# Dense products in runs of twelve, a perturbed planner, and two small edits on VectorE: one layer of a hybrid encoder on one core

## The chip, the cores and the metric

The kernel runs on one core of one Trainium2 chip. The time is device microseconds of that core. It is one launch; its engines are TensorE (PE, with its weight loads PEld), VectorE (DVE), ScalarE (ACT), GpSimd (POOL) and SyncE (SP), which issues the DMAs.

## What is computed

One layer for 1024 prompt rows and 32 sample rows (1056 columns in all), model width 1024, everything in float32. Cut to what matters:

```python
n = rmsnorm(x, norm_mix);  p = n @ w_in                  # 1024 -> 3840 columns: HGRN2 | RWKV-7
hg_o = hgrn2(p[..., :2048]);  rw_o = rwkv7(p[..., 2048:])  # the two mixers, with states
x = x + concat(hg_o, rw_o) @ w_out
x = x + cross_attend(rmsnorm(x), mk, mv) @ w_co          # mk, mv: 256 memory rows
x = x + (silu(n @ w_ff1) * (n @ w_ff3)) @ w_ff2          # n = rmsnorm(x), width 2816
y = rmsnorm(x, norm_final)
# rwkv7 begins with a shift by one row:  xs = p + (prev - p) * mu,  prev = row before
```

## The kernel before, in words

The activations lie transposed, features on the 128 partitions and the 1056 rows along the free axis, in three blocks of 352 columns.

**Dense products.** A float32 product is made of three float32r products: activations and weights are each split into a rounded part and a rest (hi, lo), and hi·hi, hi·lo and lo·hi are summed in one PSUM bank (`gemm`, line 864). `load_w` (line 850) fetches a weight tile, ScalarE rounds it (a CAST into the region `rw`), and GpSimd or VectorE subtracts to get the rest. The feed-forward stage uses seven products of sub-blocks instead of eight (`fast`, line 1252), 264 columns wide.

**The mixers.** Each 128-column tile of the projection is a dense product of 24 matmuls per block; for the 14 RWKV tiles `rw_proj` (line 1542) mixes each row with the one before it while it empties the bank. The first column of a block needs the last column of the block before, kept in a one-column tile `edge`. The mixers then work on chunks with many small products (64x64, or 128x128 blocks of which the halves are separate), between which VectorE, ScalarE and GpSimd do element-wise work; the triangular inverse (`inverse`, line 1814) is a chain of some twenty such products per piece of 256 rows.

**What sets the order.** Nothing is issued in the order of the code. The calls are recorded as nodes of a graph (`record`, line 335). Consecutive TensorE calls form one node, until `cut()` is called: `gemm` and `fast` call it every `CUT` steps of k, so a dense node has 3 x `CUT` matmuls. `plan` (line 448) is a list scheduler: it gives each node a price and walks a clock per engine, taking the ready node with the best rank; `fits` checks that tiles of SBUF (in pages of 66 words, in the regions f0, r0, rw, wr, mb, r1) and PSUM banks are there. `latest` plans backwards, and its result is the rank of the next pass. The result is one fixed order for each engine. All instructions are issued from one line of `emit`, so every row of the profile has line L378 (L383 in the changed kernel); operations are told apart by their tiles: `bank` is a PSUM bank, `rw` holds rounded weights, `wr` and `r` raw weights or rounded activations, `mb` and `f` the tiles of the mixers and other float32 tiles.

Of the kernel before, what the change touches and what calls it, by code (L numbers as in the profile page):

```python
# [33 lines left out]
CUT = 2  # L34
WARM = 2.0
LATER = 10.0
PASSES = 3
# [25 lines left out]
RESERVE = [64, 32, 24, 24, 24, 24, 24]  # L63
# [137 lines left out]
class Engine:  # L201
# [3 lines left out]
    def __getattr__(self, method):  # L205
        return lambda *args, **kw: self.graph.record(self.name, method, args, kw)

# [90 lines left out]
class Graph:  # L298
# [90 lines left out]
    def order(self):  # L389
# [7 lines left out]
        base = {n: n.cost for n in self.nodes}  # L397
        bufs = list(dict.fromkeys(b for n in self.nodes for b in n.bufs))
        best, rank = None, None
        self.log = []  # L400
        for _ in range(PASSES):
            for n in self.nodes:
                n.cost = base[n]
                if n.unit:
                    n.unit[2] = 0
            for b in bufs:
                b.at = None
            try:
                out = self.plan(rank)
            except AssertionError:  # L410
                self.log.append(None)
                break
            self.log.append(self.span)
            if best is None or self.span < best[0]:
                best = self.span, out, [b.at for b in bufs], [(n.start, n.cost) for n in self.nodes]
            rank = self.latest(out)
        self.span = best[0]
        for b, at in zip(bufs, best[2]):
            b.at = at
        for n, t in zip(self.nodes, best[3]):  # L420
            n.start, n.cost = t
        return best[1]
# [25 lines left out]
    def plan(self, rank):  # L448
# [29 lines left out]
        for n in nodes:  # L478
            n.path = n.path - n.bias if rank is None else -rank[n]
        engines = ("tensor", "vector", "scalar", "gpsimd", "sync")  # L480
        clock = dict.fromkeys(engines, 0.0)
        warm = 0.0
# [79 lines left out]
        def fits(n, start):  # L562
# [9 lines left out]
            for c in FIFO:  # L572
                k = sorted(b.turn for b in new if b.cls == c)
                if k and (k != list(range(turn[c], turn[c] + len(k))) or live[c] + len(k) > FIFO[c]):
                    return None
            ps = sum(b.space == "PS" for b in new)
            if ps:
                free = sorted(t for t in banks if t < BIG)
                if len(free) < ps + (0 if first else 2):
# [40 lines left out]
        while len(done) < len(nodes):  # L620
            turn_over()
            best = None
            for e in engines:
# [7 lines left out]
                lack = e == "tensor" and now - warm > WARM  # L631
                for t, n in sorted(ready[e], key=lambda r: (max(r[0], now), lack and not r[1].dense, -r[1].path)):
# [29 lines left out]
            if e == "tensor" and n.dense:  # L662
                warm = clock[e]
# [1389 lines left out]
```

## Time and profile before

| | |
|---|---|
| time, median of 3 runs | 1875.8 us (1875.39 to 1876.47) |
| the profiled execution's own time | 1872.31 us |
| its span, first to last instruction | 1870.6 us |
| mean granted TensorE clock | 0.988 |
| PE busy | 1798.7 us, 96% |
| VectorE, ScalarE, GpSimd busy | 69%, 44%, 32% |

The stages lie in the span like this: the input rows and first projections until about 100 us, the mixers until about 718 with the memory's keys and values behind them until 782, the output projection and cross-attention until 1136, the feed-forward hidden part until about 1600, the feed-forward output and the final norm after that. PE's busy time counts a matmul from its start to its modelled end, so a busy PE can still be switching between kinds of products or running at a lower clock.

### The profile page before, as it was taken

Reading aid. Unit: us, or ns where it says so; the run is one execution under the profiler, and the core shown is the slowest. Engines: PE = TensorE matmul, PEld = TensorE weight load, DVE = VectorE, ACT = ScalarE, POOL = GpSimd, SP = SyncE. Lnnn points to the kernel's source line nnn. Section 1 sums busy time; section 2 is a strip of 40 time slices with the busy share of each in tenths; the row PEclk is TensorE's granted clock in tenths of the full one; section 3 lists DMA queues with packets and bytes.
Section 4 is the critical chain, followed back from the end, with each engine's and each line's share of the span. In section 5 each row is a group of like instructions: output and inputs, shape, how many; then the busy total and the mean of one; then the engine's idle time right before and its main releaser. Section 6 shows DMA issues by size and latency. Waiting matters only on the chain. (4 is left out here: it accounts for less than half of the span.)

```text
span 1870.6 us, 39378 instructions
## 1 busy us (share of the span) xinstructions
PE 1798.7 (96%) x15439; PEld 1689.5 (90%) x15439; DVE 1287.8 (69%) x2547; ACT 827.0 (44%) x1938; POOL 594.7 (32%) x764
## 2 busy tenths in 40 slices
PE   6899999999999999999999999999999999999898
PEld 5898888888788888999999999899999999999897
DVE  5347746887766678623654547798877777978997
ACT  5535527465454567633322346333333333653432
POOL 6234234354323433245000024523223223233321
PEclk9999999999999999999999999999999999999999
DMA  6364123222312136844111143133222224644622
GB/s 190 103 193 113 37 79 100 81 69 64 101 49 66 61 101 193 248 139 137 47 46 46 48 149 103 46 113 123 87 94 90 87 102 169 202 146 141 194 69 94
DMA packets 206314, 201.88 MB, mean 108 GB/s; under 512 B 18712, under 2 KB 191376, under 8 KB 206128
## 3 DMA queue, kind: packets, MB, share of 16 engines
q1 hardware_dynamic: 206128, 199.37, 34.3%
q8 instruction: 121, 1.98, 0.5%
q14 instruction: 65, 0.53, 0.1%
HBM read 139.66 MB, written 59.67 MB: 107 GB/s over the span
## 5 line engine op out<-in xcount | busy, mean ns | idle before, releaser
L378 PE MATMUL bank<-r,rw 128*128 128x264 f32 (+1 forms) x5952 | 927.6, 308 | 8.9 <-DVE mb L378 4.1
L378 PEld LDWEIGHTS bank<-r,rw 128*128 128x128 f32 x5952 | 844.8, 189 | 26.6 <-issue 4.6
L378 PE MATMUL bank<-mb,rw 128*128 128x264 f32 (+2 forms) x3648 | 516.9, 296 | 17.3 <-DVE f L378 6.1
L378 PEld LDWEIGHTS bank<-mb,rw 128*128 128x128 f32 x3648 | 486.9, 190 | 25.3 <-ACT rw L378 5.7
L378 DVE TENSOR_TENSOR f<-bank,f 128x264 f32<-128x264 f32 (+6 forms) x541 | 239.6, 459 | 206.3 <-PE bank L378 167.5
L378 DVE TENSOR_TENSOR f<-f 128x264 f32<-128x264 f32 (+8 forms) x348 | 221.6, 656 | 19.1 <-POOL f L378 7.6
L378 POOL TENSOR_TENSOR f<-f 128x64 f32<-128x64 f32 (+8 forms) x237 | 128.0, 553 | 323.4 <-ACT f L378 265.2
L378 ACT CAST rw<-wr 128x512 fp32r<-128x512 f32 (+3 forms) x162 | 113.0, 705 | 242.4 <-PE bank L378 209.3
L378 PE MATMUL bank<-f 128*128 128x128 f32 (+12 forms) x1244 | 185.6, 291 | 2.5 <-DVE f L378 1.0
L378 ACT ACTIVATE f<-f 128x256 f32<-128x256 f32 (+6 forms) x331 | 142.0, 452 | 101.2 <-DVE f L378 47.9
L378 DVE TENSOR_TENSOR mb<-bank,f 128x1024 f16<-128x1024 f32 (+6 forms) x203 | 144.5, 735 | 43.8 <-PE bank L378 33.5
L378 PEld LDWEIGHTS bank<-f 128*128 128x128 f32 (+7 forms) x1244 | 141.7, 160 | 28.1 <-issue 5.5
L378 PE MATMUL bank<-f,mb 128*128 128x64 f16 (+5 forms) x2264 | 121.4, 216 | 25.5 <-POOL f L378 13.9
L378 ACT CAST rw<-r 128x512 fp32r<-128x512 f32 (+2 forms) x128 | 73.3, 574 | 121.9 <-PE bank L378 84.5
L378 ACT COPY mb<-bank 128x512 f32<-128x512 f32 (+5 forms) x175 | 76.7, 455 | 112.7 <-PE bank L378 93.6
L378 DVE TENSOR_TENSOR rw<-r,rw 128x512 fp32r<-128x512 f32 (+2 forms) x128 | 93.4, 733 | 38.0 <-ACT rw L378 37.6
L378 DVE TENSOR_TENSOR rw<-wr,rw 128x512 fp32r<-128x512 f32 (+3 forms) x132 | 102.3, 779 | 14.5 <-ACT rw L378 13.1
L378 ACT COPY f<-bank 128x264 f32<-128x264 f32 (+4 forms) x233 | 72.8, 336 | 88.7 <-PE bank L378 77.0
L378 POOL TENSOR_TENSOR r<-r 128x512 f32<-128x512 f32 (+2 forms) x45 | 66.9, 1493 | 131.9 <-DVE rw L378 67.6
L378 POOL TENSOR_TENSOR rw<-wr,rw 128x1024 fp32r<-128x1024 f32 x30 | 73.2, 2450 | 101.2 <-ACT rw L378 73.1
L378 PE MATMUL bank<-mb 64*64 64x64 f32 (+4 forms) x1556 | 84.5, 236 | 5.0 <-DVE mb L378 4.0
L378 PEld LDWEIGHTS bank<-f,mb 64*64 64x64 f32 (+3 forms) x1176 | 54.5, 139 | 34.5 <-POOL f L378 14.1
(117 smaller groups left out, 1661.6 us busy)
## 6 DMA issues: line engine op xcount, KB each, us to landing
wr<-in_w_in_dram SPq DMA_DIRECT2D x30, 512.0 KB
p_scratch<-mb SPq DMA_DIRECT2D x83, 176.0 KB
wr<-in_w_ff_dram SPq DMA_DIRECT2D x27, 512.0 KB
r<-in_w_ff_dram SPq DMA_DIRECT2D x25, 512.0 KB
f<-h_scratch SPq DMA_DIRECT2D x46, 264.0 KB
h_scratch<-f SPq DMA_DIRECT2D x17, 528.0 KB
h_scratch<-f SPq DMA_DIRECT2D x19, 396.0 KB
f<-x_scratch SPq DMA_DIRECT2D x14, 528.0 KB
```

The costliest lines, as they stand in the source:

```text
L378: getattr(eng, method)(*args, **kw)
```

## The change

Four things change.

- `CUT` goes from 2 to 4: a dense node has twelve matmuls where it had six.
- The planner: it no longer prefers a dense node when TensorE has gone more than 2 us of its clock without one (`WARM`); it no longer keeps two banks back for the oldest node; it keeps 16 pages back in the first two phases instead of 64 and 32; it makes one pass for ranks and then plans with ranks that are perturbed by fixed pseudo-random numbers (`shake`, `nudged`), instead of taking the best of three passes. `START` perturbs the first pass in the same way; each entry of `NUDGE` is a time, a seed and a reach: nodes from that time on get their rank moved by up to the reach.
- The four products `rkj` (a 128x128 constant times a per-partition factor) move from VectorE to ScalarE.
- In `rw_proj` the first column of a block is made by ScalarE alone: it scales the bank's column and adds `edge`, which now holds the previous block's last column already multiplied by `mu`. VectorE's one-column operations fall away. For the sample rows the factor is made once (`msh`, one small product).

```diff
-CUT = 2
-WARM = 2.0
+CUT = 4
-PASSES = 3
+PASSES = 1
+START, NUDGE = (291, 0.5), ((0, 3825, 0.6), (480, 1426, 0.2), (660, 4358, 1.5), (720, 1344, 0.6), (840, 6345, 3), (1200, 2280, 1.5), (1560, 9149, 3), (1620, 5315, 0.2), (1680, 6266, 12), (1740, 8928, 1.5),)
-RESERVE = [64, 32, 24, 24, 24, 24, 24]
+RESERVE = [16, 16, 24, 24, 24, 24, 24]
+def shake(i, seed):
+    return (i * 2654435761 + seed * 40503 * 65537 >> 7) % 1021 / 1020 if seed else 0.0
...
-        for _ in range(PASSES):
...
-            if best is None or self.span < best[0]:
-                best = self.span, out, [b.at for b in bufs], [(n.start, n.cost) for n in self.nodes]
-            rank = self.latest(out)
...
+        rank = None
+        for _ in range(PASSES):
+            rank = self.latest(run(rank))
+        return run(self.nudged(rank))
+
+    def nudged(self, rank):
+        out = dict(rank)
+        for at, seed, reach in NUDGE:
+            for n, t in rank.items():
+                if t >= at:
+                    out[n] = t + reach * shake(n.i, seed)
+        return out
...
-            n.path = n.path - n.bias if rank is None else -rank[n]
+            n.path = n.path - n.bias + START[1] * shake(n.i, START[0]) if rank is None else -rank[n]
...
-                if len(free) < ps + (0 if first else 2):
+                if len(free) < ps:
...
-                lack = e == "tensor" and now - warm > WARM
-                for t, n in sorted(ready[e], key=lambda r: (max(r[0], now), lack and not r[1].dense, -r[1].path)):
+                line = [(max(r[0], now), -r[1].path, r[1].i, r) for r in ready[e]]
+                line.sort()
+                for *_, (t, n) in line:
...
+        V.tensor_tensor(derived("msh", 50, 14), self.P("mu", 0, 14), self.P("sh", 0, 14), ALU.mult)
...
-            nc.vector.tensor_scalar(self.rkj[j], self.j64, self.P("rk", j), None, ALU.mult)
+            nc.scalar.activation(self.rkj[j], self.j64, AF.Copy, scale=self.P("rk", j))
...
-            S.activation(m, ps, AF.Copy, scale=self.P("omu", tile))
+            keep = self.P("omu", tile)
             c = min(TP - t0, n)
             if t0:
-                V.scalar_tensor_tensor(m[:, 0:1], edge, mu, m[:, 0:1], ALU.mult, ALU.add)
+                S.activation(m[:, 0:1], ps[:, 0:1], AF.Identity, scale=keep, bias=edge)
+                S.activation(m[:, 1:n], ps[:, 1:n], AF.Copy, scale=keep)
+            else:
+                S.activation(m, ps, AF.Copy, scale=keep)
             V.scalar_tensor_tensor(m[:, 1:c], ps[:, 0:c - 1], mu, m[:, 1:c], ALU.mult, ALU.add)
             if c == n:
                 edge = self.tmp([128, 1], "edge")
-                S.copy(edge, ps[:, n - 1:n])
+                S.activation(edge, ps[:, n - 1:n], AF.Copy, scale=mu)
             else:
...
-                V.scalar_tensor_tensor(m[:, c:c + 1], self.P("sh", tile), mu, m[:, c:c + 1], ALU.mult, ALU.add)
+                S.activation(m[:, c:c + 1], ps[:, c:c + 1], AF.Identity, scale=keep, bias=self.P("msh", tile))
```

What the planner makes of it is another order on every engine. Three places of it follow.

**VectorE near the start**, where the second batch of parameters (128x4 pieces) has just come out of a bank and the first projection tiles are mixed. Before:

```order
L378 COPY f_0_71<-bank_58 128x64
L378 TENSOR_TENSOR f_0_71<-f_0_71 128x4 x3
L378 TENSOR_SCALAR f_0_71<-f_0_71 128x4 x4
L378 TENSOR_SCALAR f_0_71<-f_0_71 128x128 x4
L378 SCALAR_TENSOR_TENSOR mb_87<-bank_60,f_0_71,mb_87 128x319
L378 SCALAR_TENSOR_TENSOR mb_87<-bank_60,f_0_71,mb_87 128x31
L378 SCALAR_TENSOR_TENSOR mb_87<-f_0_71,mb_87 128x1 x2
```

In the changed kernel:

```order
L383 SCALAR_TENSOR_TENSOR mb_87<-bank_61,f_0_71,mb_87 128x351
L383 COPY f_0_71<-bank_60 128x64
L383 TENSOR_SCALAR f_0_71<-f_0_71 128x4 x4
L383 SCALAR_TENSOR_TENSOR mb_87<-bank_64,f_0_71,mb_87 128x319
L383 SCALAR_TENSOR_TENSOR mb_87<-bank_64,f_0_71,mb_87 128x31
L383 TENSOR_TENSOR f_0_71<-f_0_71 128x4 x4
```

The four 128x128 products (`rkj`) are gone from ahead of the mixing that empties the banks, and so are the one-column operations behind it.

**PE at the end of the mixers**, where the last projection products (`r`, `rw`) stand between the small products of the last RWKV pieces and HGRN blocks. Before:

```order
L378 MATMUL bank_61<-r_0_79,rw_83 128x352
L378 MATMUL bank_61<-r_0_91,rw_83 128x352
L378 MATMUL bank_61<-r_0_79,rw_83 128x352 x2
L378 MATMUL bank_61<-r_0_91,rw_83 128x352
L378 MATMUL bank_61<-r_0_79,rw_83 128x352
L378 MATMUL bank_64<-f_0_71 128x128
L378 MATMUL bank_64<-f_0_71 32x32 x2
L378 MATMUL bank_64<-f_0_71 64x64
L378 MATMUL bank_62<-r_0_79,rw_83 128x352
L378 MATMUL bank_62<-r_0_91,rw_83 128x352
```

In the changed kernel, from the stretch behind its last projection product:

```order
L383 MATMUL bank_64<-f_0_71 128x128
L383 MATMUL bank_64<-f_0_71,mb_87 128x128
L383 MATMUL bank_63<-f_0_71,mb_87 64x64 x4
L383 MATMUL bank_65<-f_0_71 32x32
L383 MATMUL bank_60<-mb_87,f_0_71 128x64
L383 MATMUL bank_62<-f_0_71,mb_87 64x64 x4
L383 MATMUL bank_61<-f_0_71 128x128
L383 MATMUL bank_61<-mb_87 32x32 x2
L383 MATMUL bank_61<-mb_87 64x64
```

Before, dense runs of six stand between groups of small products until late in the mixers; in the changed kernel the last projection product is issued while more of the mixers' small work is left, and small products follow each other from there on.

**ScalarE at the turn from attention to the feed-forward stage**: `128x352` is the last norm, `128x1056` the two first sigmoids, a CAST into `rw` rounds feed-forward weights. Before:

```order
L378 ACTIVATE f_0_71<-f_0_71 128x352 x6
L378 CAST rw_83<-f_0_71 128x512
L378 ACT_TABLE_LOAD
L378 ACTIVATE f_0_71<-r_1_11985 128x1056 x2
L378 CAST rw_83<-wr_75 128x512
L378 CAST rw_83<-f_0_71 128x512
L378 CAST rw_83<-wr_75 128x512 x3
```

In the changed kernel:

```order
L383 ACTIVATE f_0_71<-f_0_71 128x352 x5
L383 CAST rw_83<-f_0_71 128x512
L383 ACTIVATE f_0_71<-f_0_71 128x352
L383 CAST rw_83<-wr_75 128x512
L383 CAST rw_83<-f_0_71 128x512
L383 COPY f_0_71<-bank_58 128x264
L383 CAST rw_83<-wr_75 128x512
L383 COPY f_0_71<-bank_62 128x264
L383 ACT_TABLE_LOAD
L383 ACTIVATE f_0_71<-r_1_11989 128x1056
L383 CAST rw_83<-wr_75 128x512 x2
```

Four casts now stand ahead of the first sigmoid instead of one, and the second sigmoid no longer follows the first directly.

More of the change, by code (lines that the diff above doesn't have):

```diff
@@ L396, in order, with run @@
                     n.preds.update({p: None for p in min(later, key=lambda u: u.i).preds if p.calls[0][0] != "memset"})
[L397 to L400, printed above, removed]
-        for _ in range(PASSES):
-            for n in self.nodes:
+        base = {n: n.cost for n in nodes}
+        bufs = list(dict.fromkeys(b for n in nodes for b in n.bufs))
+        def run(rank):
+            for n in nodes:
                 n.cost = base[n]
@@ L407, in order @@
                 b.at = None
[L408 to L413, printed above, removed]
-            if best is None or self.span < best[0]:
-                best = self.span, out, [b.at for b in bufs], [(n.start, n.cost) for n in self.nodes]
-            rank = self.latest(out)
[L417 to L422, printed above, removed]
+            return self.plan(rank)
+        rank = None
[9 more added lines that the diff above has]
+        return out
     def latest(self, out):
@@ L478, in plan @@
         for n in nodes:
-            n.path = n.path - n.bias if rank is None else -rank[n]
+            n.path = n.path - n.bias + START[1] * shake(n.i, START[0]) if rank is None else -rank[n]
         engines = ("tensor", "vector", "scalar", "gpsimd", "sync")
         clock = dict.fromkeys(engines, 0.0)
-        warm = 0.0
         port = 0.0
@@ L571, in fits @@
                 return start
[L572 to L575, printed above, removed]
+            for c in {b.cls for b in new}:
+                if c in FIFO:
+                    k = sorted(b.turn for b in new if b.cls == c)
+                    if k != list(range(turn[c], turn[c] + len(k))) or live[c] + len(k) > FIFO[c]:
+                        return None
             ps = sum(b.space == "PS" for b in new)
@@ L661, in plan @@
             clock[e] = start + n.cost
-            if e == "tensor" and n.dense:
-                warm = clock[e]
             if n.port:
```

## The prediction

> **What bounds the kernel now.** I read the page's first part, then stretches of the span cut where the program's stages change, then what TensorE (PE) waited for, then single places in the timeline. The columns of a stretch are its length, then busy time and instruction count of PE, weight load, VectorE (DVE), ScalarE (ACT) and GpSimd (POOL), then the granted clock, the DMA share and GB/s.
>
> ```profile
> PE 1798.7 (96%) x15439; PEld 1689.5 (90%) x15439; DVE 1287.8 (69%) x2547; ACT 827.0 (44%) x1938; POOL 594.7 (32%) x764
> ...
> 42.00:100.00 58.00, 52.82 (x324) 51.38 (x325) 21.05 (x57) 30.61 (x69) 10.56 (x9) 0.94 0.38 117
> 100.00:640.00 540.00, 524.02 (x5646) 456.12 (x5646) 363.85 (x737) 268.63 (x657) 206.42 (x291) 0.99 0.28 82
> ...
> 682.80:717.60 34.80, 31.60 (x390) 24.70 (x388) 29.71 (x113) 27.31 (x108) 14.79 (x44) 0.95 0.41 118
> ...
> 1136.00:1212.00 76.00, 67.82 (x509) 66.25 (x508) 60.44 (x99) 42.42 (x104) 39.34 (x35) 0.93 0.22 65
> 1212.00:1600.00 388.00, 387.23 (x3173) 386.84 (x3172) 312.69 (x484) 127.94 (x232) 113.41 (x76) 1.00 0.32 107
> ...
> 1740.00:1790.00 50.00, 44.22 (x344) 43.16 (x343) 47.70 (x108) 17.51 (x40) 20.09 (x23) 0.97 0.53 172
> ```
>
> PE is the bound nearly everywhere: 72 of 1870.6 us idle, and none at all in the middle of the feed-forward stage (0.77 of 388 us). Its arithmetic does not change, so a gain can only come from idle time, from switching between kinds of product, or from a reduced clock. Idle time sits in the mixer stage (16 us of 100 to 640), its tail, the turn from attention to feed-forward (8.2 us of 1136 to 1212), the end, and the first 42 us, where the change leaves the order nearly as it was. What PE waited for is mostly VectorE:
>
> ```profile
> PE bank L378 <- DVE mb L378: 12.8, 10, 4.1
> PE bank L378 <- DVE f L378: 9.7, 8, 2.6
> PE bank L378 <- ACT mb L378: 8.0, 7, 3.6
> ```
>
> A wait of two microseconds costs twice, because after it PE runs at half its granted clock for a stretch (the number before the DMA share); ahead of the stretches stand two such waits, in brackets:
>
> ```profile
> 236.31 0.52 PE L378 MATMUL bank<-mb,f 64*64 64x64 f32 x8 [2.02 <-DVE mb L378]
> 697.44 0.22 PE L378 MATMUL bank<-f,mb 128*128 128x64 f16 x2 [0.94 <-DVE f L378]
> ...
> 60.60:67.40 6.80, 5.22 (x18) 5.22 (x19) 2.89 (x14) 5.26 (x11) 1.05 (x4) 0.50 0.65 201
> 237.90:241.50 3.60, 3.60 (x24) 2.96 (x24) 3.51 (x5) 0.26 (x1) 3.44 (x4) 0.53 0.24 55
> 333.60:337.00 3.40, 3.40 (x18) 3.33 (x14) 3.40 (x8) 0.45 (x1) 1.68 (x5) 0.51 0.00 0
> 514.50:521.40 6.90, 5.24 (x34) 4.42 (x34) 2.98 (x7) 4.73 (x10) 1.78 (x2) 0.51 0.25 66
> 698.90:702.30 3.40, 3.34 (x42) 2.88 (x42) 3.33 (x12) 3.01 (x13) 0.40 (x2) 0.50 0.37 120
> 1204.00:1210.90 6.90, 5.83 (x25) 5.52 (x26) 5.90 (x9) 1.89 (x4) 3.05 (x2) 0.51 0.27 78
> ```
>
> **Term 1, fewer switches: -10 us.** Counted over the whole order of PE, the dense products (float32r) stand in 289 unbroken runs before and in 188 after; changes of the array's shape (a 64-row or 64-column product next to a full one) fall from 430 to 397, because the dense runs lose 82 of them (201 to 119) while the small products among themselves gain 49. The prices:
>
> ```profile
> 45.12 9.91 PE L378 MATMUL bank<-r,rw 128*128 128x352 f32 x60
> 54.96 0.27 PE L378 MATMUL bank<-f 64*128 64x64 f32 x1
> ...
> 197.73 1.21 PE L378 MATMUL bank<-r,rw 128*128 128x352 f32 x6
> 198.78 0.41 PE L378 MATMUL bank<-f,mb 128*128 128x64 f16 x8
> ...
> 265.44 2.20 PE L378 MATMUL bank<-r,rw 128*128 128x352 f32 x12
> 267.57 0.65 PE L378 MATMUL bank<-f,mb 64*128 64x64 f32 x14
> ```
>
> Sixty products take 9.84 us from start to start, and with the two edges below off, 0.161 us each. Six of them between full-size products take 1.05 us, 0.08 more than 6 x 0.161: the first load of weights is not hidden. Twelve that are followed by a 64-row product take 2.13 us, 0.20 more than 1.93: the same 0.08 and some 0.1 for the change of shape. So 101 x 0.08 + 33 x 0.1 = 11.4 us; I take 10, since not every run restarts in the open; bounds 8 and 11.4.
>
> **Term 2, the start: -6 us.** Four products `rkj` move from VectorE to ScalarE.
>
> ```profile
> L378 DVE TENSOR_SCALAR f<-f 128x128 f32<-128x128 f32 x4 | 5.1, 1333 | 0.0
> ...
> 55.10 2.00 ACT L378 CAST rw<-wr 128x1024 fp32r<-128x1024 f32 x2
> 56.22 4.75 POOL L378 TENSOR_TENSOR rw<-wr,rw 128x1024 fp32r<-128x1024 f32 x2 [18.71 <-ACT rw L378]
> 61.17 0.69 DVE L378 SCALAR_TENSOR_TENSOR mb<-bank,f,mb 128x319 f32<-128x319 f32 x2
> 62.18 2.13 PE L378 MATMUL bank<-r,rw 128*128 128x352 f32 x6 [4.07 <-DVE mb L378]
> ```
>
> They took 5.1 us, beside two large GpSimd subtractions, and the operations that empty the PSUM banks (61.17) stood behind them; PE idled 4.07 us and then ran from 62.18 to 67.4 at half clock, six products in 2.13 us instead of 1.05, which loses 2.6 more: 6.7 us at stake. The next weights would also have been late: their cast (1.0) and subtraction (2.4) start when the last pair of weights is used up, at 55, so with VectorE out of the way PE could start at 58.6. In the new order the first of the two weight tiles is used up 24 products, 3.9 us, earlier, which covers those 3.4 us. I take 6; bounds 0 (the weights become the wait) and 6.7. On ScalarE the four cost little: a cast four times as wide takes 0.60 there (1203.72, below), and the engine is 44% busy.
>
> The first-column edit goes the same way:
>
> ```profile
> L378 DVE SCALAR_TENSOR_TENSOR mb<-f,mb 128x1 f32<-128x1 f32 x42 | 14.7, 378 | 0.0
> L378 ACT COPY f<-bank 128x1 f32<-128x1 f32 x56 | 7.2, 167 | 8.6 <-DVE mb L378 5.5 <-POOL f L378 2.8
> ```
>
> VectorE loses 42 operations, 14.7 us, and ScalarE gains 42 of one column, some 7 us at 0.167, spread over the projections beside PE. By themselves I count them as nothing; if a bank waited for each, it would be those 7 us. What they give is room on VectorE, which is in term 3.
>
> **Term 3, stalls inside the mixers: -8 us.** At stake are the 16 us idle and about 6 us for half clock (13.9 us at half, less the idle time within). I traced each PE step back through the new and the old order to the PE step that it depends on, and compared the PE work that lies between with the mean durations on the way. Of the steps in this stage those with under 1 us to spare fall from 145 to 63. A static order meets durations that vary, so few spare microseconds are where it stalls. I take 40% of 22 us, rounded down; bounds -18 and +5, since the planner now holds no bank and fewer pages back, so that a step can also find its bank taken, a wait that this trace does not show apart.
>
> **Term 4, the mixers' tail: +11 us.** The new order uses the dense projections up earlier. I sum PE's work there over the order, each pair of neighbours at the median start-to-start time that such a pair has in the trace. Before, from the last projection product to the first memory product PE has 27 us of small work, the stretch 682.8 to 717.6 above: 34.8 us long, VectorE busy 29.71 of it (85%). After, the same stretch holds 59 us of PE work, with a whole triangular inverse in it, and 202 VectorE operations instead of 115. At the mean durations of their kinds these sum to 86 us against 39, for instance ten of
>
> ```profile
> L378 DVE TENSOR_TENSOR mb<-bank,f 128x1024 f16<-128x1024 f32 x10 | 12.2, 1220 | 5.5 <-PE bank L378 4.3 <-ACT f L378 1.3
> ```
>
> Records overlap: 29.71 busy for a sum of 39 is 0.77, so 66 us busy, and at 85% the stretch lasts 77 us, 18 over PE's work, against 7.5 over it now: +10.5. VectorE becomes the bound here. Bounds 0 (it is as well fed as at 1740 to 1790, 95%, and earlier stages hand it less) and +20.
>
> **Term 5, the turn to feed-forward: -5 us.** Here weight casts stood on ScalarE behind two sigmoids that wait for VectorE:
>
> ```profile
> 1194.64 0.60 ACT L378 CAST rw<-f 128x512 fp32r<-128x512 f32 x1
> ...
> 1201.56 2.26 ACT L378 ACTIVATE f<-r 128x1056 f32<-128x1056 f32 x2 [5.02 <-DVE r L378]
> 1203.72 0.60 ACT L378 CAST rw<-wr 128x512 fp32r<-128x512 f32 x1
> 1204.38 0.81 PE L378 MATMUL bank<-mb,rw 128*128 128x264 f32 x2 [3.55 <-ACT rw L378]
> ```
>
> The wait and the half clock after it (6.9 us at 0.51, where some 2.7 us are lost) make 6.3 us. In the new order four casts stand between the normalisation and the first sigmoid, and three between the two. Bounds 0 (VectorE, 60.44 of 76 us busy here, supplies the other half of the same weights) and -7.
>
> The rest: the feed-forward pieces double too, but there a run is not broken. At the end VectorE is 95% busy and its work stays the same: 0, give or take 4. One table load (of six) goes, off the path.
>
> **The sum** is -10 - 6 - 8 + 11 - 5 = -18 against the profiled execution's 1872.3 us (span 1870.6 and 1.7 around it): 1854.3. The three timed runs have their median 3.5 above the profiled one, so I add that: 1858.
>
> **The rivals.** *The clock falls in the tail (slower).* The old rule put a dense product first once PE had gone 2 us without one; it is gone, and the new order has small products for 59 us in a row and for 7 to 11 us in seven other places. If such stretches lower the clock as idle time does, the 59 us run at 0.5 and take 118 instead of 77: +41, 1899. It decides once the clock there averages under 59/95 = 0.62, where the whole gain is gone. For it: the half-clock stretch at 698.9 lies inside the one long stretch without dense work, after only 0.94 us idle. Against it: the other nine tenths of that stretch ran at full clock. The Trainium skill ("TensorE: Matmul & The Clock Gate", Parts 1 and 4) says that the clock halves after an idle window of about 3.4 us and that transposes do not count as busy in the same way, which speaks against the change. By that rule the sum goes towards this rival's 1899 where transposes fill a window, and by the row at 682.8 it stays at 1858; the trace agrees on the length of the stretches (3.4 and 6.8 us) but shows them after idle gaps of 2 us too. *Slack is worth nothing.* The mixers stall as often as now, the turn's wait moves to VectorE, and the tail comes near its upper bound, +17: -10 - 6 + 17 = +1, so 1877, no change. For it: what stalls is a chain of VectorE operations slowed beside GpSimd, which no order removes. *The tail is hidden.* Earlier stages leave VectorE less to catch up on and most stalls go: -10 - 6 - 14 + 2 - 6 = -34: 1842.
>
> **How the numbers follow.** Forecast 0.62, hidden tail 0.16, slack worth nothing 0.12, clock 0.10. 0.2% is about what a measurement of this kernel can tell from no change: under 1872.0 is faster, over 1879.6 slower. The forecast's own spread (terms 3 and 4, about 10 us) gives 1844 to 1872. Faster: nearly all of the first two and a quarter of the third (0.61 + 0.16 + 0.03), 0.80; same 0.10; slower 0.10. For 8 times in 10 the range takes in half of the hidden-tail case and the case of no change: 1840 to 1876.
>
> **What would show it.** Right: no half-clock stretch near 60 us and the first long dense run without a wait; PE idle under 12 us in the mixers; a tail of about 77 us, VectorE over 80% busy; no ScalarE wait at the turn. Wrong: a granted clock near 0.6 in the tail, or idle time in the mixers as now. Then the term named is wrong.

## The result, and the profile after

The changed kernel takes 1831.5 us (median of four runs, 1827.1 to 1835.8) against 1875.6 us for the kernel before: the ratio is 0.977 with a 95% interval of 0.974 to 0.980. The forecast was 1858 us, -18; the change brought -44. Beside the later runs the kernel before took 1870.8 to 1872.9 us, so there the gain is some 40. The profiled execution took 1828.0 us (span 1826.2).

To see where the time went I use the sum of term 4 for the whole program: PE's order, each pair of neighbours at its median price in the trace of before. That is PE's **work**. What an execution takes beyond it is **lost** (waits, reduced clock), and the losses are read off by stages of that work. With these prices the work falls from 1748.7 to 1739.2 us. Work and loss are thus worked out and not measured; only their sum is.

| stage (PE's work, us) | lost before | lost after | difference | forecast |
|---|---|---|---|---|
| start (0-100) | 32.6 | 23.5 | -9.1 | -6 (term 2) |
| mixers (100-576) | 34.3 | 19.0 | -15.3 | -8 (term 3) |
| mixers' tail (576-700) | 12.7 | 24.9 | +12.2 | +11 (term 4) |
| memory, cross-attention (700-1050) | 6.7 | 2.1 | -4.6 | 0 |
| turn to feed-forward (1050-1176) | 14.6 | 2.9 | -11.7 | -5 (term 5) |
| feed-forward (1176-1501) | 0.0 | -0.4 | -0.4 | 0 |
| end | 13.3 | 6.7 | -6.6 | 0 |
| PE's work | | | -9.5 | -10 (term 1) |

The differences make -45.0 us up to the start of PE's last product. The 27 us that were not forecast are 11.6 in stages that were put at nothing, 7.3 in the mixers, 6.7 at the turn and 3.1 at the start, less 0.5 of work and 1.2 of tail. The split depends on the prices: with medians over each three neighbours, pooled over all twenty traces, the work falls by 5.9 us and the mixers and the tail change by -16.8 and +10.0; the other stages come out within 0.5 us of the table.

The page's line of busy times, of the changed kernel:

```profile
PE 1779.5 (97%) x15439; PEld 1681.4 (92%) x15439; DVE 1264.6 (69%) x2502; ACT 836.3 (46%) x1983; POOL 605.7 (33%) x764
```

PE is idle for 47 of the span's 1826.2 us, 72 before. Its stretches (same columns as before the change) that answer to those of the prediction:

```profile
42.00:100.00 58.00, 57.18 (x360) 56.13 (x359) 16.48 (x43) 31.37 (x83) 13.00 (x10) 1.00 0.27 82
...
100.00:640.00 540.00, 535.11 (x5947) 474.79 (x5946) 368.18 (x752) 293.51 (x730) 216.99 (x317) 1.00 0.30 90
...
622.80:706.40 83.60, 75.72 (x925) 60.44 (x923) 71.87 (x198) 55.38 (x180) 32.13 (x81) 0.84 0.41 117
...
1100.00:1180.00 80.00, 79.09 (x639) 78.17 (x638) 63.41 (x113) 47.68 (x114) 49.84 (x38) 1.00 0.25 78
...
1697.00:1747.00 50.00, 48.59 (x391) 47.82 (x390) 49.90 (x119) 20.81 (x48) 19.07 (x22) 1.00 0.46 145
```

The last line is the part of the program that lay at 1740 to 1790 before, where PE was busy for 44.22 us. The start and the turn run nearly without a gap, the end with 1.4 us of idle time in these 50 instead of 5.8, and the mixers have 4.9 us of idle PE where they had 16. The tail is the exception: 83.6 us at a mean clock of 0.84. Its inside, in the stretches of another cut:

```profile
620.00:651.70 31.70, 29.91 (x452) 24.83 (x452) 29.84 (x63) 21.42 (x57) 12.95 (x26) 1.00 0.52 146
651.70:679.00 27.30, 23.89 (x178) 19.02 (x177) 18.59 (x61) 12.53 (x47) 9.06 (x32) 0.50 0.39 104
679.00:700.00 21.00, 18.68 (x253) 14.10 (x253) 20.00 (x66) 19.95 (x65) 10.68 (x24) 1.00 0.28 87
```

For 27.3 us in a row PE runs at half clock although it is busy for 23.89 of them. Before, the longest such stretch within the program was 6.8 us. The waits of PE, where the longest of 12.3 us is the program's own beginning:

```profile
PE bank L383 <- DVE mb L383: 18.3, 10, 12.3
PE bank L383 <- DVE f L383: 4.9, 10, 1.1
...
PE bank L383 <- ACT mb L383: 3.3, 6, 1.0
```

### The profile page after: what moved, and what is told of

Same layout as the page of the kernel before. It is cut to its first block, busy times and chain, and to the rows that moved or that the text cites. A ratio compares the mean times of both kernels' runs of the same rounds, so it can differ in the third digit from the quotient of the medians.

```text
span 1826.2 us, 39245 instructions
## 1 busy us (share of the span) xinstructions
PE 1779.5 (97%) x15439; PEld 1681.4 (92%) x15439; DVE 1264.6 (69%) x2502; ACT 836.3 (46%) x1983; POOL 605.7 (33%) x764
## 4 chain that ended last, share of the span: by engine, by line
PE 83%; DVE 5%; ACT 3%; DMA 2%; issue 1%; POOL 1%; SPq 0%; DVEq 0%; POOLq 0%; ACTq 0%
PE bank L383 83%; DVE f L383 2%; DVE mb L383 2%; ACT mb L383 2%; ACT f L383 1%; DVE rw L383 1%; DVE r L383 1%; DMA f<-p_scratch 1%; POOL mb L383 0%; ACT r L383 0%; POOL f L383 0%; ACT rw L383 0%; DMA f<-h_scratch 0%; DMA x_scratch<-mb 0%; DMA f<-in_cache_mem_k_dram 0%
## 5 line engine op out<-in xcount | busy, mean ns | idle before, releaser
L383 PE MATMUL bank<-r,rw 128*128 128x264 f32 (+1 forms) x5928 | 894.7, 305 | 4.3 <-POOL rw L383 2.0
L383 PEld LDWEIGHTS bank<-r,rw 128*128 128x128 f32 x5928 | 837.1, 188 | 13.3 <-POOL rw L383 3.2
L383 PE MATMUL bank<-mb,rw 128*128 128x264 f32 (+4 forms) x3672 | 509.6, 293 | 4.8 <-DVE r L383 1.9
L383 POOL TENSOR_TENSOR f<-f 128x64 f32<-128x64 f32 (+8 forms) x205 | 115.4, 572 | 330.5 <-PE bank L383 187.8
L383 DVE TENSOR_TENSOR f<-f 128x264 f32<-128x264 f32 (+8 forms) x309 | 188.5, 626 | 20.2 <-ACT f L383 13.1
L383 ACT ACTIVATE f<-f 128x256 f32<-128x256 f32 (+7 forms) x295 | 124.5, 447 | 114.0 <-DVE f L383 61.6
L383 DVE TENSOR_TENSOR mb<-bank,f 128x1024 f16<-128x1024 f32 (+6 forms) x200 | 135.8, 705 | 44.5 <-PE bank L383 35.6
L383 PE MATMUL bank<-f,mb 64*64 64x64 f32 (+5 forms) x2248 | 122.9, 221 | 21.9 <-DVE mb L383 17.9
L383 ACT COPY f<-bank 128x264 f32<-128x264 f32 (+8 forms) x221 | 76.0, 359 | 60.3 <-PE bank L383 44.9
L383 DVE TENSOR_TENSOR rw<-r,rw 128x512 fp32r<-128x512 f32 (+2 forms) x106 | 80.0, 755 | 23.0 <-ACT rw L383 22.2
L383 ACT ACTIVATE mb<-bank,f 128x1 f32<-128x1 f32 (+5 forms) x133 | 55.4, 461 | 48.5 <-PE bank L383 45.5
L383 PE MATMUL bank<-mb 64*64 64x64 f32 (+5 forms) x1310 | 76.0, 237 | 1.1 <-ACT mb L383 1.0
```

The costliest lines, as they stand in the source:

```text
L383: getattr(eng, method)(*args, **kw)
```

## The experiments

The first reading of the two traces left two theories. *A: the order itself.* Each set of ranks gives one order out of many, here called a draw. A stall sits where this one order happens to be late, in every stage; the perturbed ranks moved that, and what the edits and the longer runs do is small beside it. *B: the parts.* VectorE, freed of 46 operations, or the long dense runs let PE go through. All runs, with lost time by stage from one profiled execution each (for the runs with added products the work includes them):

| kernel | median us | ratio to before, 95% | work | start | mixers | tail | turn | end |
|---|---|---|---|---|---|---|---|---|
| changed, side by side with e17, e18 (e16) | 1831.5 | 0.977-0.980 | 1739.2 | 23.0 | 20.4 | 25.0 | 3.5 | 9.1 |
| before, two edits only (e1) | 1888.4 | 1.007-1.011 | 1743.1 | 39.2 | 28.4 | 32.0 | 14.5 | 14.0 |
| before, runs of twelve only (e2) | 1926.7 | 1.028-1.031 | 1734.5 | 34.0 | 48.1 | 78.9 | 10.9 | 8.0 |
| changed, no seeds (e3) | 1874.5 | 1.000-1.002 | 1738.3 | 36.4 | 28.7 | 35.6 | 12.5 | 9.8 |
| changed, other seeds (e4) | 1871.0 | 0.999-1.002 | 1734.5 | 30.4 | 12.9 | 53.9 | 3.4 | 17.2 |
| before, order kept, `rkj` on ScalarE (e5) | 1870.8 | 0.998-1.001 | 1748.7 | 32.7 | 36.3 | 12.7 | 15.8 | 13.7 |
| changed, order kept, `rkj` on VectorE (e6) | 1836.9 | 0.979-0.984 | 1739.2 | 24.9 | 19.8 | 24.8 | 8.5 | 8.1 |
| changed, tail filled to 659 us (e7) | 1832.3 | 0.977-0.981 | 1742.0 | 23.6 | 20.3 | 21.6 | 2.9 | 12.3 |
| changed, no seeds, runs of six (e8) | 1873.2 | 1.000-1.002 | 1748.6 | 49.5 | 20.5 | 14.2 | 10.0 | 14.0 |
| changed, START only (e9) | 1854.2 | 0.989-0.992 | 1737.7 | 23.9 | 20.4 | 45.0 | 1.9 | 11.9 |
| and nudges at 0, 480 (e10) | 1846.2 | 0.984-0.988 | 1738.5 | 23.4 | 19.6 | 35.2 | 1.9 | 12.9 |
| and at 660, 720 (e11) | 1837.0 | 0.980-0.983 | 1739.4 | 24.1 | 20.9 | 25.1 | 2.0 | 12.5 |
| and at 840, 1200 (e12) | 1832.5 | 0.978-0.981 | 1739.2 | 23.2 | 19.6 | 28.4 | 2.6 | 11.3 |
| changed, tail filled through (e13) | 1826.6 | 0.973-0.977 | 1742.5 | 23.5 | 19.3 | 15.8 | 2.7 | 8.3 |
| the same again (e17) | 1829.9 | 0.975-0.980 | 1742.5 | 24.3 | 19.4 | 15.3 | 2.7 | 8.5 |
| and the start filled (e18) | 1826.8 | 0.974-0.978 | 1744.2 | 21.6 | 21.0 | 19.3 | 2.9 | 8.9 |
| before, drawn with seed 291 (e14) | 1903.6 | 1.013-1.019 | 1746.4 | 28.9 | 29.5 | 44.8 | 12.4 | 14.3 |
| before, drawn with seed 7 (e15) | 1935.4 | 1.031-1.036 | 1745.6 | 30.0 | 47.4 | 40.2 | 26.6 | 19.6 |

One split in this table is not borne out by its trace, that of e4. With the pooled prices named above its mixers lose 20.0 us and its tail 28.5, against 10.1 and 20.5 in the changed kernel. For the other kernels these prices put some 3 to 10 us less into the mixers (17 for e2) and at most 8 less into the tail.

### One part alone in the kernel before

The first run has only the two ScalarE edits (the `rkj` and the first-column hunks of the change, with `msh`); the planner and its numbers are the old ones, but since its nodes differ it finds another order.

```diff
-nc.vector.tensor_scalar(self.rkj[j], self.j64, self.P("rk", j), None, ALU.mult)
+nc.scalar.activation(self.rkj[j], self.j64, AF.Copy, scale=self.P("rk", j))
...
-V.scalar_tensor_tensor(m[:, 0:1], edge, mu, m[:, 0:1], ALU.mult, ALU.add)
+S.activation(m[:, 0:1], ps[:, 0:1], AF.Identity, scale=keep, bias=edge)
```

> The old planner and its old numbers, with the two ScalarE edits alone (rkj and the first column). Theory A (the gain beyond the forecast comes from the order: stalls of PE and the half-clock stretches after them go in the mixers, at the turn and at the end): the edits give the start at most, so 1869 to 1876 us, with the stall at the turn (some 14 us lost there) still in place. Rival B (VectorE, freed of 46 operations and some 20 us, is what lets PE run through): at least half of the 44 us, under 1855.

The second has only the longer runs:

```diff
-CUT = 2
+CUT = 4
```

> The kernel before with the dense products in runs of twelve, nothing else. Theory A: the switches go (8 to 11 us), and what the longer runs do to the rest of the order is of either sign, since the tail loses its dense products: 1860 to 1875. Rival C (the long runs themselves keep PE fed): under 1850, with under 3 us lost at the turn.

Both made the kernel slower, by 0.9% and 3.0%. Neither part brings the gain by itself, so theory B falls in both forms. What a part is worth these two runs do not tell, because each also found a new order. Theory A's numbers were missed too, for I had not expected that a mere new order could cost 15 to 55 us. In e1 the turn loses 14.5 us as before. In e2 nearly all of it is the mixers and their tail (+14 and +66 us): the dense products are gone early, and the tail spends long stretches at half clock, the longest of which is this one:

```profile
664.90:688.80 23.90, 14.64 (x139) 12.06 (x137) 19.16 (x35) 8.88 (x23) 4.21 (x14) 0.50 0.06 19
```

### The seeds

```diff
-START, NUDGE = (291, 0.5), ((0, 3825, 0.6), (480, 1426, 0.2), ...)
+START, NUDGE = (0, 0.0), ()
```

> The changed kernel without any perturbation of the ranks. If the planner's settings and the edits carry the gain, 1828 to 1840 us; if the ten chosen seeds carry what went beyond the forecast (theory A in its narrow form), 1845 to 1862, with stalls and half-clock stretches back at the turn and at the end.

```diff
-START, NUDGE = (291, 0.5), ((0, 3825, 0.6), (480, 1426, 0.2), ...)
+START, NUDGE = (2291, 0.5), ((0, 5825, 0.6), (480, 3426, 0.2), ...)
```

> The changed kernel with every seed number raised by 2000, reaches and places kept. If any perturbation does as well, within 5 us of 1831; if the chosen ten matter, as without seeds: 1845 to 1862. The difference to the run without seeds shows how much one draw of an order moves the time.

Without perturbed ranks, and with other seeds, the changed kernel takes what the kernel before takes: ratios 1.001 and 1.000. This was worse than theory A said (1845 to 1862): the chosen seeds carry not only what went beyond the forecast but the whole gain. The two differ in where they lose. In the stretches of the run without seeds the half-clock tail and the stalled turn are plain:

```profile
42.00:100.00 58.00, 51.55 (x319) 49.86 (x319) 17.48 (x43) 31.85 (x79) 10.38 (x9) 0.94 0.37 116
...
660.00:720.00 60.00, 49.36 (x579) 39.93 (x579) 49.82 (x130) 36.96 (x111) 22.32 (x57) 0.68 0.16 42
674.88:705.60 30.72, 24.68 (x204) 20.95 (x205) 25.24 (x61) 15.57 (x53) 8.19 (x27) 0.50 0.19 53
...
1194.00:1215.00 21.00, 13.78 (x94) 13.60 (x94) 17.97 (x27) 7.30 (x12) 5.00 (x3) 0.76 0.09 25
```

The wait at the turn, in PE's timeline of that run:

```profile
1198.71 3.10 PE L383 MATMUL bank<-mb,rw 128*128 128x264 f32 x24
1209.03 5.47 PE L383 MATMUL bank<-r,rw 128*128 128x264 f32 x24 [7.22 <-DVE f L383]
```

With the other seeds the mixers stall as well, with 14.2 us of idle time in PE and 17 us at half clock, where the changed kernel has 4.9 and none:

```profile
100.00:626.00 526.00, 511.75 (x5513) 454.79 (x5515) 359.32 (x711) 278.68 (x703) 208.76 (x303) 0.98 0.30 87
```

Then the nudges were put back from the front: first none, then two, four, six of the ten.

```diff
 START, NUDGE = (291, 0.5), (
+(0, 3825, 0.6), (480, 1426, 0.2),
+(660, 4358, 1.5), (720, 1344, 0.6),
+(840, 6345, 3), (1200, 2280, 1.5),
 )
```

> The changed kernel with the first seed (START) kept and none of the ten nudges. Theory A': each stage has stalls by the draw of its order, and each nudge was picked for what follows it; so the start up to PE's first differing product stays as it was and every later stage is as without seeds: 1860 to 1876. Rival (START sets the tone and the nudges are trimmings): under 1840.

> The nudges at 0 and 480 kept, the later eight left out. PE's products are in the changed kernel's order for the first 578 us of its work, so up to there the time lost matches it (42.5 us lost at 576, within 3); behind it the mixers' tail, the turn and the end are ordinary draws: tail 25 to 36 us lost instead of 24.9, turn 9 to 15 instead of 3, end 6 to 13 instead of 4.5, together 1842 to 1866. Rival (the early draw is what counts): under 1838.

> The nudges at 0, 480, 660 and 720 kept; PE's order is the changed kernel's for the first 818 us of work. The tail stays as it is in the changed kernel (65 to 70 us lost by 700); the turn and the end are ordinary draws: 8 to 20 us more, 1839 to 1852. Rival (nothing behind the mixers is of weight): within 3 us of 1831.

> The nudges up to 1200 kept, the four at 1560, 1620, 1680 and 1740 left out. Only the end can differ: it loses 6 to 13 us instead of 4.5, so 1832 to 1840. Rival (the end stays as it is, since the products there stand in the same order): within 2 us of 1831.

1854.2, 1846.2, 1837.0 and 1832.5 us: each pair takes some off, and START takes 20. But the places are not those of my list. START cleared the start, the mixers and also the turn, which I had given to the later nudges (expected 9 to 15 us lost there, measured 1.9); it made the tail worse (45.0 against 35.6). The nudges at 0 and 480 and those at 660 and 720 then took 10 us each off the tail. The next two and the last four move 4.5 and 1 us, near or below the spread of the executions: with PE's products in the same order up to the tail's end, e11, e12 and the changed kernel lose 25.1, 28.4 and 24.9 us in it.

### Runs of six or twelve

```diff
 (no seeds)
-CUT = 4
+CUT = 2
```

> The changed kernel without perturbed ranks and with runs of six again, beside the run without perturbed ranks (1874.5). Term 1: the switches come back, 9 to 11 us more work for PE. Term 4: the mixers' tail keeps its dense products and loses 12 to 20 us instead of the 35 it lost there, so 15 to 23 us less. Together 1861 to 1870. Rival (which stage stalls is a matter of the single order, whatever the length of the runs): the tail's loss is as large as with runs of twelve, and the time above 1876.

By the prices of term 1 the work is 10.3 us more (which counts the switches again and does not measure them), and the tail loses 14.2 us instead of 35.6. The total was expected 5 to 13 us lower and is the same within 1.3 us, since this order happens to lose 13 us more at the start, most of it in one wait:

```profile
57.06 1.97 PE L383 MATMUL bank<-f,mb 128*128 128x128 f32 x16
68.71 2.36 PE L383 MATMUL bank<-f,mb 128*128 128x128 f32 x8 [9.68 <-ACT mb L383]
```

In this pair of orders the longer runs take about as much as they give: at most 10 us of switches against about 20 in the tail. That the length of the runs is the cause is not shown, for runs of six lose 40 to 45 us in the tail in two other orders (e14, e15). (Term 1's price is itself uncertain: with the prices of the changed kernel's trace the work falls by 3.7 us instead of 9.5, with prices pooled over eight executions by 5.5. No run measures it alone.)

### The four products on VectorE, with the order held

The order is planned as always, and only then the engine of the four operations is exchanged:

```diff
+if out.buf.name == "rkj":   # after order(), before emitting
+    node.eng, node.calls = "scalar", [("activation", (out, src, AF.Copy), dict(scale=mul))]
```

> The order of the kernel before, kept to the last instruction, with only the four rkj products moved from VectorE to ScalarE at their places. Term 2 of the prediction: the wait of 4.07 us near 60 us and the half clock after it go, so 4 to 6.7 us less. Rival (the order of the products there, with the weights used up earlier, made the gain, and the four operations had no part): no change, the wait still there, released by VectorE or by the weights.

The reverse, in the order of the changed kernel, is the second run.

> The order of the changed kernel, kept, with only the four rkj products put back on VectorE. Term 2: a wait and a half-clock stretch near 60 us come back, 4 to 6.7 us more. Rival: the new order does not need VectorE at that place, and nothing changes (within 1 us).

Term 2's mechanism falls twice. In the old order the four operations on ScalarE changed nothing: 32.7 us lost at the start instead of 32.6. PE still waits, now 3.21 us and for ScalarE:

```profile
57.61 1.97 PE L382 MATMUL bank<-f,mb 128*128 128x128 f32 x16
62.79 3.59 PE L382 MATMUL bank<-r,rw 128*128 128x352 f32 x12 [3.21 <-ACT f L382]
```

The reason stands in ScalarE's timeline of that run, and VectorE's:

```profile
56.58 2.00 ACT L382 CAST rw<-wr 128x1024 fp32r<-128x1024 f32 x2
58.47 0.98 ACT L382 ACTIVATE f<-f 128x128 f32<-128x128 f32 x3
59.36 0.54 ACT L382 ACTIVATE mb<-bank,f 128x352 f32<-128x352 f32 x1
```

```profile
59.93 0.71 DVE L382 SCALAR_TENSOR_TENSOR mb<-bank,f,mb 128x319 f32<-128x319 f32 x2 [2.20 <-ACT mb L382]
60.56 1.96 DVE L382 SCALAR_TENSOR_TENSOR mb<-f,mb 128x1 f32<-128x1 f32 x2
```

The operations that empty the banks begin on ScalarE, and there the moved products now stand ahead of them, 0.39 us each, with the casts; VectorE waits 2.20 us for them. Then VectorE is late itself once more: its first one-column operation takes 1.83 us, where the second takes 0.2. It runs beside one of GpSimd's two subtractions, as two of the four products did in the kernel before, which took 2.40 and 2.38 us where the other two took 0.28 each. The first line is from the kernel before, the others are from this run:

```profile
56.36 2.40 DVE L378 TENSOR_SCALAR f<-f 128x128 f32<-128x128 f32 x1
...
57.70 4.67 POOL L382 TENSOR_TENSOR rw<-wr,rw 128x1024 fp32r<-128x1024 f32 x2 [20.31 <-ACT rw L382]
60.56 1.83 DVE L382 SCALAR_TENSOR_TENSOR mb<-f,mb 128x1 f32<-128x1 f32 x1
```

In each case VectorE's operation ends within 0.1 us of the subtraction, so I take GpSimd for what held it (the last section counts such cases). Then the 5.1 us of term 2 were for the most part GpSimd's time, and taking the four products away hands the block on to the next operation. ScalarE would not have been ready much sooner, as a table load and two small operations hold its copies until 62.5. I had followed the wait one step back and not two. In the new order PE has its long dense run there on either account; PE's timeline of e6, with the products on VectorE:

```profile
54.55 0.22 PE L387 MATMUL bank<-f 64*128 64x64 f32 x1
54.69 11.47 PE L387 MATMUL bank<-r,rw 128*128 128x352 f32 x70
```

The start loses 24.9 us with them on VectorE and 23.0 to 23.5 without, so they are worth at most 1 to 2 us of the 9 gained there. e6 takes 5.5 us more in all; most of that is one wait at the turn in its one profiled execution (3.93 us instead of 0.9 and 1.5 in two of the changed kernel; 8.5 us lost there instead of 2.9 and 3.5), far from the exchanged operations. What made it longer is open. The first-column edit was not tried with the order held, and the planner's new numbers were not tried one by one.

### The clock in the tail

In every trace the half-clock stretches last 3.41 us or a multiple of it (but for the one cut off at the end), and all start on one grid of 3.41 us, whose phase differs from execution to execution. I therefore counted, for each slice of the grid, what PE did in it and at which clock the next slice ran. PE's busy time does not separate them well. The number of columns that its products streamed does (at least 64 counted for a product; a 128x352 product has 352): in the first six traces a mark of 2376 columns in a slice puts 3207 of 3233 slices on the right side, whether the clock of the slice itself was full or half. At half clock small products can stay under the mark although PE is busy, while dense products get over it even then (one in 0.29 us in the kernel before at 24 us, so some 4100 columns in a slice). In the changed kernel the slice from 648.29 us has 2112 columns and the seven behind it 1024 to 2176, although PE is busy throughout most of them. What ends such a stretch the mark does not tell: the eighth slice has 1792 columns, and full clock follows. The test adds columns without changing the order:

```diff
+reps = {669: 2, 671: 3, 672: 3, 674: 3, 675: 3, 676: 3, 680: 2}  # k-th TensorE node of the order
+node.calls = node.calls * reps[k]
```

> The order of the changed kernel, kept, in which seven small groups of products between 649 and 663 us are computed two or three times over (the same eight fp16 products into the same place: some 2.8 us more work for PE, half of it in its gaps). In the six traces so far nearly every 3.41 us slice in which PE streamed under some 2400 columns (at least 64 counted for a product) is followed by one at half clock, whatever the clock was, and the changed kernel is at half clock from 651.7 to 679.0 us. Theory D (the clock falls on too few columns, and at half clock small products cannot get over that mark again): the 27 us stretch stays at full clock, 6 to 12 us less. Rival (VectorE bounds the tail, the clock costs nothing there): 0 to 3 us more. Rival (the clock follows something else, such as the kind of product): the stretch is at half clock as before, 1 to 5 us more.

> As the run that computed seven groups of the tail twice or three times over, with one more group (at 662 us) computed four times instead of twice. There the clock held through 649 to 659 us, where the added products had lifted each 3.41 us slice over 2800 columns, and fell to half behind the first slice under the mark of some 2300 to 2400 (659.4 us, 2176 columns) for 13.7 us. Theory D: with some 1000 columns more in that slice the half-clock stretch goes altogether, and with it 4 to 6 us in the tail against that run; total 1824 to 1831. Rival (the chain through VectorE sets the tail's length): the stretch goes and the tail is not shorter.

In e7 the clock held through the filled slices (2880 to 4864 columns) and fell behind the first that was not filled enough (2176), for 13.7 us. In e13, with that group computed four times, it held throughout. The same stretches as shown for the changed kernel, in e13:

```profile
620.00:651.70 31.70, 30.18 (x463) 25.27 (x462) 28.56 (x62) 21.36 (x58) 13.36 (x26) 1.00 0.51 153
651.70:679.00 27.30, 23.72 (x407) 19.89 (x404) 24.35 (x84) 18.28 (x67) 12.59 (x36) 1.00 0.42 112
...
623.10:699.90 76.80, 69.04 (x1036) 55.94 (x1035) 70.24 (x198) 55.55 (x179) 32.91 (x81) 1.00 0.44 127
```

In the same 27.3 us PE now does 407 products, the added ones among them, instead of 178, and VectorE is busy for 24.35 us instead of 18.59; the whole stretch without dense products lasts 76.8 us instead of 83.6, with 3.3 us more work in it. So theory D and its rival hold in turn: at half clock PE holds this place up, and at full clock VectorE, busy for 70.24 of 76.8 us (91%), is the likely bound. The total of e7 did not move (1832.3 us, where 6 to 12 less were expected); that of e13 is 1826.6. To price it the kernels were timed side by side:

> The changed kernel itself, as the measure for the two runs beside it: 1827 to 1836 us, a half-clock stretch of 20 to 30 us in the tail.

> The tail with the added products once more, timed on the same chip as the changed kernel. Theory D (half clock makes the tail long): 4 to 7 us under the changed kernel, as its tail lost 13.2 us of 576 to 651 instead of 23.2, with 3.3 us of added work. Rival (1826.6 against 1831.5 was the chip of the day): within 2 us of it.

```diff
-reps = {..., 680: 4}
+reps = {..., 680: 4, 5: 5}    # and the transposes at 16.7 us
```

> As that run, with one group of transposes at 16.7 us computed five times over, ahead of the 2.4 us in which PE waits for the first rows and behind which it runs 3.4 us at half clock. Theory D: the stretch at 20 us goes and with it up to 1.7 us; the added transposes lie in the wait. Rival (the added work delays the rows or the transposes behind it): 0 to 2 us more.

The tail's gain is there again in e17 (15.3 us lost against 25.0), but its total, 1829.9 us (1825.1 to 1834.9), is not told apart from 1831.5 (1830.4 to 1832.1), and 4 to 7 us less were expected. e18 is at 1826.8 us (1825.5 to 1829.4): all five of its runs lie under all four of the changed kernel on the same chip, by 4.7 us in the middle. Its stretch at 20 us went, but one at 26 us came: that part did as little as its rival said. Filling the tail thus shortens it in all three traces (to 77, 77 and 80 us, from 84 in both of the changed kernel). In the total that shows clearly in e18 alone, the fastest version timed beside the changed kernel.

### Two draws of the planner before

```diff
-n.path = n.path - n.bias if rank is None else -rank[n]
+n.path = n.path - n.bias + 0.5 * shake(n.i, 291) if rank is None else -rank[n]
```

> The kernel before, planner and code, with its first ranks perturbed by seed 291 and reach 0.5 as START does. Theory A' (the order of the moment decides, in the planner before as in the changed one): the time moves by several us to either side: 1850 to 1895. Rival (it takes the changed planner's numbers to gain or lose by a draw): within 5 us of 1873.

> The same with seed 7, a number picked for nothing: a second draw of the planner before, 1850 to 1895 by theory A', within 5 us of 1873 by the rival.

Ranks that differ by at most 0.5 us move the time by +31 and +63 us, more than any range I had given, and both upwards. The planner before has thus four other orders in this study, at 1888 (edits), 1904, 1927 (runs of twelve) and 1935 us; its own 1873 is the best of five. The changed planner without the chosen seeds gave 1871, 1873 (runs of six) and 1874. That may mean that its numbers make a poor order less likely; with so few draws, and edits mixed in, it is a hint and not shown.

## Why the prediction was wrong, point by point

The forecast treated the new order as the old one with some of its stalls removed. It is another draw, and its seeds are worth the whole 40 us: without them, or with other ones, nothing is left of the gain. (That they were picked by trying is how they look; no run shows it.) In the sum the largest misses are the rest, put at 0 for -11.6, term 3 and term 5.

- **Term 1** (-10): -9.5 with the prices it was made with, and 10.3 between e3 and e8 with the same prices. Right in count; the price (3.7 to 9.5 in all) was not measured apart.
- **Term 2** (-6): the start gained 9.1 us, 5.8 of it at the place I named (26 to 51 us of work), but for another reason. The step that failed is "with VectorE out of the way PE could start at 58.6": with the four products moved and the order kept it started at 62.79 (e5, which is 1.5 us late by then). What stood in the way was for the most part VectorE held beside GpSimd's subtractions, and not the products' own 0.28 us each. The order decides it: e2, with the old planner, runs of twelve and the four products still on VectorE, loses 0.2 us between 26 and 51 us of work, where the kernel before loses 6.9.
- **Term 3** (-8): the mixers gained 15.3 us. The step that failed is the 40%, and its ground, the count of PE steps with under 1 us to spare. Counted in the same way for other orders it says nothing: 145 steps and 34.3 us lost before, 63 and 19.0 after; but 54 and 28.7 without seeds, and 133 and 20.5 with runs of six.
- **Term 4** (+11): +12.2, and in its parts closer than it deserved. The stretch lasts 83.6 us where 77 was predicted, 7 of them from the half clock that the term left to a rival. At full clock (e13) it lasts 76.8, and that is luck, since two misses cancel: VectorE was busy for 70.24 us instead of 66, and for 91% of the stretch instead of 85%. What the term missed is that the tail is the most variable stage: 12.7 to 78.9 us over the orders of this study.
- **Term 5** (-5): -11.7. Mis-sized: only the wait at 1204 us and its half clock were put at stake, 6.3 us, while the stage had 14.6 us to lose. The trace of before shows another half-clock stretch at 1152.87, which is missing from the list of the prediction and was not priced:

```profile
1152.80:1156.30 3.50, 3.50 (x18) 3.50 (x17) 3.50 (x11) 3.44 (x10) 0.00 (x0) 0.51 0.37 127
```

- **The rest** (0, give or take 4): -11.6 (cross-attention -4.6, end -6.6, feed-forward -0.4). Putting it at nothing is the step that cost most. "At the end VectorE is 95% busy" was a wrong ground for it: at the same place of the changed kernel VectorE is busy for 49.90 of 50 us and PE idles 1.4 us instead of 5.8. The cross-attention, with 6.7 us to lose, was not looked at.
- **The rivals.** *The clock falls in the tail* was right as a mechanism and small in effect: 27 us at half clock, a mean of 0.84 where 0.62 would have undone the gain. *Slack is worth nothing* comes near in number to the order without seeds, 1874.5 against the 1877 worked out for it, though its stalls lie elsewhere. *The tail is hidden* did not happen.
- **What would show it** did show: no half clock near 60 us, 4.9 us idle in the mixers, VectorE 86% busy in the tail, at the turn one wait for ScalarE of 0.9 us. The tail took 83.6 us instead of about 77. Nearly all of this came true and the total was still wrong, because they asked only whether stalls go, and not how many stages had some.

## What to carry to other kernels

Where a scheduler decides the order, a change of its inputs is a new draw before it is anything else: ask first how far draws spread (here 1831 to 1935 us), and test an edit with the order held. What another order can gain, beside fewer switches, is to be looked for in all of the lost time in the trace, stage by stage (here 114 us), not only in the stalls whose cause one recognises. A stretch of small products can drop the clock, and the clock can then stay down for many slices; columns streamed per slice told better than busy time where it falls. And where an operation is slow, look at what runs beside it before moving it.

## What the runs showed of the hardware

- The granted clock changes in slices of 3.41 us on a fixed grid. Over all twenty traces, 259 of 10,682 slices were followed by one at half clock; the mark of 2376 columns, taken from the first six, names 217 of them and 35 others (219 and 51 when a product is counted in the slice in which it starts). The best mark on PE's busy time (54% of the slice) names 127 and 23 others. So the columns carry most of it, but not all; other sums over a slice were not tried. Transposes count: with the products' own columns the first six traces leave 26 slices on the wrong side of the best mark, and 49 when those of transposes are left out. (The Trainium skill, "TensorE: Matmul & The Clock Gate", Part 4, has transposes not counting as busy in the same way; here the measurement decides.)
- Part 1 of the same page of the Trainium skill describes an activity window that runs freely and a fall after an idle window of about 3.4 us. The traces agree on the length of the slice and on its running free of the program; they differ on the idle window, for the slice ahead of the 27.3 us stretch was busy for 2.29 of 3.41 us:

```profile
648.29:651.70 3.41, 2.29 (x29) 1.60 (x27) 3.37 (x6) 3.26 (x12) 0.96 (x1) 1.00 0.93 243
```

- A half-clock stretch can be far longer than the gap that begins it: 27.3 us after gaps of at most 0.56 us, and in the first draw of the planner before (e14) this one, with PE busy for four fifths of it:

```profile
674.00:721.80 47.80, 38.98 (x358) 31.11 (x355) 35.42 (x92) 25.61 (x82) 16.13 (x44) 0.50 0.21 59
```

- The grid's phase differs between executions, and so can decide over a half-clock stretch. The changed kernel has one at 1806 us in one of its two profiled executions and not in the other, although PE waits 0.52 and then 1.31 us there in both: in the one with it (e16) both waits fall into one slice, in the other into two. This is one source of the spread of some 0.3%; that it is the only one was not tested.
- An operation of VectorE whose operands are all in SBUF can be held by a subtraction of GpSimd and end with it: 0.28 us became 2.40 and 2.38 in the kernel before and 1.13 in e6, and 0.2 became 1.83 in e5. Over all twenty traces 644 such operations began well within a GpSimd tensor_tensor of over 1.5 us, and 385 of them took at least 0.4 us longer than the fastest fifth of their kind. Of 1326 operations that read a PSUM bank and began there, none did. No run was made to test it.
